# One inverse square root for the norms of four heads' queries and keys

## The chip, the cores and the metric

The kernel runs on one core of one Trainium2 chip. The metric is the time of one execution on the device, in microseconds (us). Five engines matter: PE (TensorE, the matrix engine; PEld is its weight load), DVE (VectorE), ACT (ScalarE), POOL (GpSimd) and SP (SyncE, which here only issues DMA transfers). Each engine works through its own instructions in order, and semaphores between them carry the dependences.

## The reference

The reference is an encoder trunk on 512 positions of width 1024 in float32, with two layers. Layer 0 is a state-space mixer (S5) and a SwiGLU feed-forward block of inner width 2816. Layer 1 has latent attention (MLA) as its mixer, "the second mixer", and another such block. Every block is preceded by an RMS norm that is modulated by a conditioning vector. The part that the change touches is how the attention's heads are made:

```
q = rms_norm(h @ w_dq, q_norm_g) @ w_uq            # 16 heads, 64 + 32 columns each
q_nope = rms_norm(q_nope, q_nope_norm_g)           # over 64 columns of one head
q_rope = apply_rope(rms_norm(q_rope, ...), cos, sin)  # over 32 columns of one head
kv = (c_kv @ w_kv_b)                               # 16 heads, 64 key + 64 value columns
k_nope = rms_norm(k_nope, k_nope_norm_g)           # over 64 columns of one head
rms_norm(x, g) = x * rsqrt(mean(x * x) + 1e-6) * g
```

The scores are masked in chunks of 64 positions, a softmax follows, and the weighted values go through an output projection. For each position and head there are thus three inverse square roots of a mean: of the query's 64 columns, of its 32 rotary columns, and of the key's 64 columns.

## The kernel before

Positions lie in four tiles of 128 partitions. The 16 heads are handled in four groups of four. Products are taken in three passes on PE (high by high, high by low, low by high; `mm3`, lines 923 to 925), so each operand is split into a high part (a cast on ACT) and a low part (a subtraction on DVE, or on POOL for the weights of the head projections, line 164).

The mixer is `mla` (line 1327). A prologue makes the first group: `project` loads its weights, `project_q` and `project_k` multiply and add up squares (DVE reduces at lines 1470, 1471 and 1448, into `hss`), `rotate_q` rotates the raw rotary columns on POOL, `norm_q` and `norm_k` normalize, and `turn` transposes each head's tile on PE and splits it (ACT line 1508, DVE line 1510). In the prologue the two multiplies by the inverse roots of the 64-column norms run on DVE, the rotary one on POOL.

Then a loop over n = 0 to 16 handles one head in each pass. `scores` multiplies queries by keys (PE, lines 1525 to 1527), takes a row minimum on DVE (line 1529) and the exponential on ACT (1530). `scale` divides the rows (DVE 1543, ACT 1541). `spread` transposes the head before and splits it (ACT 930, DVE 931), and `weigh` multiplies it by the values. Into these passes `fill` puts the making of the next group. In its first pass (h = 0, at the end of the pass) come `project`, four `project_q`, `rotate_q` and `norm_q`. In the second pass (h = 1, in front of `weigh`) come four `project_k` and `norm_k`. The third and fourth pass turn the queries and keys. In the loop all three norm multiplies run on POOL (line 158 is the shared helper of multiplies). Group 1 is made beside the attention of group 0, and so on; the traces below have group 1 from about 637 to 679 us, group 2 to 723 us, group 3 to 748 us.

`rsqrt` (line 214) is an inverse square root in integer and float steps on DVE: the mean plus epsilon into `var` (line 1475, once for each kind of norm), a shift (225), a subtraction from a constant (226), and three Newton steps of three instructions (229 to 231). That is 2 + 9 = 11 instructions beside the averages. `norm_q` does it on 32 columns (16 pairs of tile and head, 64-column and rotary norm), `norm_k` on 16. Their scratch tiles come from a pool with one buffer for each tag, "hq" and "hk".

The order of work on each engine is set by a planner when the kernel is built: it takes the instructions with their dependences and places them by its own estimate of their times, so the instructions of one norm stand between those of other work. Besides the data dependences, `issue_after(ins)` puts instructions behind `ins` in their engine's order. `fill` uses it with `self.last`, the rotary multiply of the last query norm: POOL's weight splits of the next group stand behind it. `self.normed` is the last 64-column multiply, used the same way in the prologue.

Of the kernel before, what the change touches and what calls it, by code (L numbers as in the profile page):

```python
# [11 lines left out]
F32 = mybir.dt.float32  # L12
F32R = mybir.dt.float32r
I32 = mybir.dt.int32
# [4 lines left out]
P = 128  # L19
# [6 lines left out]
NOPE = 64  # L26
ROPE = 32
VD = 64
QK = NOPE + ROPE
# [26 lines left out]
class Trunk:  # L56
# [154 lines left out]
        v.tensor_scalar(out=c, in0=cm1, scalar1=1.0, scalar2=None, op0=ALU.add)  # L211
        return s, c, cm1

    def rsqrt(self, pool, ss, n, inv_d, tag):

        v = self.nc.vector
        var = pool.tile([P, n], F32, tag=tag + "v", name=self.name("var"))
        sh = pool.tile([P, n], I32, tag=tag + "s", name=self.name("sh"))
        y = pool.tile([P, n], I32, tag=tag + "y", name=self.name("y"))
        t = pool.tile([P, n], F32, tag=tag + "t", name=self.name("t"))  # L220
        if callable(ss):
            ss(var)
        else:
            v.tensor_scalar(out=var, in0=ss, scalar1=inv_d, scalar2=EPS, op0=ALU.mult, op1=ALU.add)
        v.tensor_scalar(out=sh, in0=var.bitcast(I32), scalar1=1, scalar2=None, op0=ALU.logical_shift_right)
        v.tensor_scalar(out=y, in0=sh, scalar1=-1, scalar2=0x5F3759DF, op0=ALU.mult, op1=ALU.add)
        yf = y.bitcast(F32)
        for _ in range(3):
            v.tensor_tensor(out=t, in0=yf, in1=yf, op=ALU.mult)
            v.scalar_tensor_tensor(out=t, in0=t, scalar=-0.5, in1=var, op0=ALU.mult, op1=ALU.mult)  # L230
            v.scalar_tensor_tensor(out=yf, in0=t, scalar=1.5, in1=yf, op0=ALU.add, op1=ALU.mult)
        return yf
# [1169 lines left out]

    def fill(self, q, h):

        g = self.nc.gpsimd
        if q > 3:
            return
        if h == 0:
            with self.tc.issue_after(self.last.ins):
                self.project(q)  # L1410
            for t in range(4):
                self.project_q(q, t)
            rot = self.tmp.tile([P, 4, 4, ROPE], F32, tag="t0", name=self.name("rot"))
            self.rotate_q(rot)
            self.last = self.norm_q(g, rot)
        elif h == 1:
            for t in range(4):
                self.project_k(q, t)
            self.norm_k(g)
        else:  # L1420
            for j, i in ((0, 1), (1, 1), (2, 1)) if h == 2 else ((0, 0), (1, 0), (2, 0), (3, 1), (3, 0)):
                self.turn(j, i)
# [53 lines left out]
                                            in1=eps.unsqueeze(2).to_broadcast([P, 4, 4]), op0=ALU.mult, op1=ALU.add)  # L1476

    def norm_k(self, eng):
        r = self.rsqrt(self.sm, lambda var: self.mean(var, self.hss[:, 0], self.eps[0], NOPE), 16, None, "hk")
        kn = self.ktm.rearrange("a t h c -> a (t h) c")[:, :, 0:NOPE]  # L1480
        self.normed = self.mul(eng, kn, kn, r.unsqueeze(2).to_broadcast([P, 16, NOPE])).ins

# [3 lines left out]
    def norm_q(self, eng, rot):  # L1486
        v, g = self.nc.vector, self.nc.gpsimd
        qtm, ss = self.qtm, self.hss

        def var(t):  # L1490
            for i, n in enumerate((NOPE, ROPE)):
                self.mean(t[:, 16 * i:16 * i + 16], ss[:, 1 + i], self.eps[1], n)

        r = self.rsqrt(self.sm, var, 32, None, "hq")
        q4 = qtm.rearrange("a t h c -> a (t h) c")
        rb = lambda o, c: r[:, o:o + 16].unsqueeze(2).to_broadcast([P, 16, c])
        self.normed = self.mul(eng, q4[:, :, 0:NOPE], q4[:, :, 0:NOPE], rb(0, NOPE)).ins
        return self.mul(g, q4[:, :, NOPE:QK], rot.rearrange("a t h c -> a (t h) c"), rb(16, ROPE))

    def turn(self, h, i, behind=None):  # L1500

        nc, v = self.nc, self.nc.vector
        src, g = ((self.ktm, self.gk), (self.qtm, self.gq))[i]
        pt = self.ps()
        for t in range(4):
            self.transpose(pt[0:QK, t * P:(t + 1) * P], src[:, t, h], self.ident)
        hi, lo = self.heads[h][i]
        self.last_turn = nc.scalar.activation(out=hi[0:QK], in_=pt[0:QK], func=AF.Copy, scale=g)
        with self.after(behind):
            v.scalar_tensor_tensor(out=lo, in0=pt[0:QK], scalar=g, in1=hi[0:QK].bitcast(F32), op0=ALU.mult, op1=ALU.subtract)  # L1510
# [120 lines left out]
```

## Time and profile before

| | |
|---|---|
| median of 3 runs | 1204.1 us (1202.7 to 1206.66) |
| the profiled execution | 1201.67 us |
| its span, first to last instruction | 1199.9 us |
| mean granted TensorE clock | 0.971 |
| PE, DVE, ACT, POOL busy | 1131.3, 754.3, 491.3, 154.7 us |

The page gives averages over the whole span. A stretch of the span has its own limits, so a row by stretch gives the busy time of each engine in it, beside its length. A group's row adds up the busy time of like instructions: the mean against the time of the shortest tells how much of it is waiting inside instructions. Timelines give single instructions in order: start, duration, engine and line; in brackets, the engine's idle time in front of it and what ended it.

### The profile page before, as it was taken

How to read it: one execution, taken by the hardware profiler on the slowest of the kernel's cores; microseconds unless marked ns; L12 is line 12 of the kernel's file. 1: busy time of each engine (PE TensorE's matmuls, PEld its weight loads, DVE VectorE, ACT ScalarE, POOL GpSimd, SP SyncE). 2: the span in 40 equal slices, each digit the busy share in tenths (PEclk: the TensorE clock that was granted, in tenths of full speed). 3: DMA queues.
4: the chain of work that ended last, by engine and by line, in shares of the span. 5: the costliest groups of instructions: out<-in, count | busy, mean ns of one | idle time of the engine just before them, and what ended most of it. 6: DMA issues, size and time to landing. Idle time of an engine off the chain costs nothing.

```text
span 1199.9 us, 18340 instructions
## 1 busy us (share of the span) xinstructions
PE 1131.3 (94%) x7030; PEld 954.1 (80%) x7030; DVE 754.3 (63%) x1472; ACT 491.3 (41%) x913; POOL 154.7 (13%) x191
## 2 busy tenths in 40 slices
PE   4787898999999999999978988999999999999998
PEld 2565788987777787789967867899978888888888
DVE  8877378598888733756689889768843333322223
ACT  4641465322222322234676868644422322322222
POOL 5997000000000000000143233000000000000000
PEclk7888998999999999999988989999999999999999
DMA  9589965278788732635401021045633333333343
GB/s 266 194 192 198 215 180 157 83 251 260 248 275 261 242 100 84 200 112 173 123 31 36 1 71 36 1 142 167 189 103 102 88 91 103 88 88 104 107 116 105
DMA packets 230072, 167.49 MB, mean 140 GB/s; under 512 B 9776, under 2 KB 204256, under 8 KB 229984
## 3 DMA queue, kind: packets, MB, share of 16 engines
q1 hardware_dynamic: 208904, 128.47, 38.6%
q10 hardware_dynamic: 21080, 37.85, 9.4%
q8 instruction: 55, 0.90, 0.3%
q14 instruction: 33, 0.27, 0.1%
HBM read 163.21 MB, written 3.08 MB: 139 GB/s over the span
## 4 chain that ended last, share of the span: by engine, by line
PE 84%; DVE 9%; ACT 3%; DMA 3%; issue 1%; POOL 0%; SPq 0%; ACTq 0%; DVEq 0%
PE ps L923 24%; PE ps L924 24%; PE ps L925 24%; PE ps L146 2%; DMA a<-in_x 1%; PE ad L811 1%; DVE a L161 1%; DMA adaw<-in_ada_w 1%; PE ac L301 1%; DVE a L158 1%; PE po L924 1%; ACT a L930 1%; PE po L925 1%; DVE a L931 1%; DVE mn L1529 1%
## 5 line engine op out<-in xcount | busy, mean ns | idle before, releaser
L923 PE MATMUL ps<-a,wh 128*128 128x512 f32 (+1 forms) x1406 | 490.0, 353 | 3.7 <-ACT a L996 3.7
L924 PE MATMUL ps<-a,wh 128*128 128x512 f32 (+1 forms) x1406 | 492.2, 352 | 0.6 <-DVE a L997 0.6
L925 PE MATMUL ps<-a,wl 128*128 128x512 f32 (+1 forms) x1406 | 492.3, 352 | 0.0
L912 ACT CAST wh<-raw 128x1024 fp32r<-128x1024 f32 (+1 forms) x179 | 182.6, 1023 | 500.0 <-PE ps L924 359.0
L164 DVE TENSOR_TENSOR wl<-raw,wh 128x1024 fp32r<-128x1024 f32 x173 | 206.6, 1195 | 195.8 <-ACT wh L912 192.5
L923 PEld LDWEIGHTS ps<-a,wh 128*128 128x128 f32 x1406 | 262.9, 189 | 47.0 <-ACT a L996 4.7
L924 PEld LDWEIGHTS ps<-a,wh 128*128 128x128 f32 x1406 | 265.4, 189 | 40.0 <-DVE a L997 0.9
L925 PEld LDWEIGHTS ps<-a,wl 128*128 128x128 f32 x1406 | 265.0, 189 | 39.3 <-DVE wl L164 0.2
L350 DVE SCALAR_TENSOR_TENSOR acc<-a,csil,acc 128x512 f32<-128x512 f32 x126 | 94.5, 750 | 32.4 <-DMA a<-in_ada_w 23.8
L1115 DVE TENSOR_TENSOR si<-si,ps 128x512 f32<-128x512 f32 x44 | 30.1, 685 | 77.4 <-PE ps L925 74.5
L164 POOL TENSOR_TENSOR a<-raw,a 128x768 fp32r<-128x768 f32 (+1 forms) x2 | 4.7, 2356 | 470.1 <-ACT a L912 470.1
L146 PE MATMUL ps<-ident,a 128*128 128x128 f32 (+1 forms) x304 | 47.6, 298 | 18.4 <-POOL a L158 6.6
L146 PEld LDWEIGHTS ps<-ident,a 128*128 128x128 f32 (+1 forms) x304 | 38.1, 146 | 26.1 <-POOL a L158 7.3
L1003 DVE SCALAR_TENSOR_TENSOR xT<-ps,mod,xT 128x256 f32<-128x256 f32 (+1 forms) x35 | 20.4, 583 | 44.5 <-PE ps L925 44.4
L1530 ACT ACTIVATE a<-ps,mn 128x128 f32<-128x128 f32 (+1 forms) x64 | 34.1, 539 | 14.7 <-DVE mn L1529 14.5
L924 PE MATMUL ps<-a,a 128*128 128x256 f32 (+2 forms) x108 | 33.5, 311 | 0.0
L923 PE MATMUL ps<-wh,a 128*128 128x288 f32 (+3 forms) x100 | 33.2, 334 | 0.2 <-DVE a L931 0.2
L923 PE MATMUL ps<-a,a 128*128 128x256 f32 (+2 forms) x108 | 33.1, 313 | 0.0
L1529 DVE TENSOR_REDUCE mn<-ps 128x1 f32<-128x128 f32 (+1 forms) x64 | 30.2, 482 | 4.6 <-PE ps L1527 4.5
L925 PE MATMUL ps<-a,a 128*128 128x256 f32 (+2 forms) x108 | 32.8, 311 | 0.0
L925 PE MATMUL ps<-wh,a 128*128 128x288 f32 (+3 forms) x100 | 32.6, 328 | 0.0
L924 PE MATMUL ps<-wl,a 128*128 128x288 f32 (+3 forms) x100 | 32.4, 325 | 0.0
(324 smaller groups left out, 1458.0 us busy)
## 6 DMA issues: line engine op xcount, KB each, us to landing
a<-in_ada_w ACTq DMA_DIRECT2D x112, 256.0 KB, 4.2
raw<-in_ffn_w_gate SPq DMA_DIRECT2D x44, 512.0 KB, 4.0
raw<-in_ffn_w_up SPq DMA_DIRECT2D x44, 512.0 KB, 5.9
raw<-in_ffn_w_down SPq DMA_DIRECT2D x42, 512.0 KB, 3.8
adaw<-in_ada_w SPq DMA_DIRECT2D x24, 512.0 KB, 8.0
a<-in_ada_w SPq DMA_DIRECT2D x16, 512.0 KB, 7.3
a<-in_kv_ada_w ACTq DMA_DIRECT2D x32, 256.0 KB, 4.1
raw<-in_ffn_w_down SPq DMA_DIRECT2D x21, 384.0 KB, 3.3
```

The lines of the kernel that those rows point to most:

```text
L146: self.nc.tensor.transpose(out=out, in_=in_, identity=ident)
L158: return eng.tensor_tensor(out=out, in0=a, in1=b, op=ALU.mult)
L164: eng.tensor_tensor(out=out, in0=a, in1=b, op=ALU.subtract)
L350: v.scalar_tensor_tensor(out=acc, in0=x, scalar=self.csil[:, k:k + 1], in1=acc, op0=ALU.mult, op1=ALU.add)
L912: nc.scalar.copy(out=flat(wh), in_=flat(raw))
L923: mm(out, lhsT=lhs[0], rhs=rhs[0], start=start, stop=False)
L924: mm(out, lhsT=lhs[0], rhs=rhs[1], start=False, stop=False)
L925: self.last_mm = mm(out, lhsT=lhs[1], rhs=rhs[0], start=False, stop=stop).ins
L1003: self.nc.vector.scalar_tensor_tensor(out=self.xT[:, m, sl], in0=src, scalar=gate[:, m:m + 1], in1=self.xT[:, m, sl], op0=ALU.mult, op1=AL ...
L1115: nc.vector.tensor_tensor(out=t, in0=t, in1=pp[i][1], op=ALU.mult)
L1529: v.tensor_reduce(out=mn[:, t:t + 1], in_=pt, axis=AX.X, op=ALU.min)
L1530: nc.scalar.activation(out=p[:, self.OFF[t]:self.OFF[t] + w], in_=pt, func=AF.Exp, scale=-1.0, bias=mn[:, t:t + 1], accum_out=su[:, t:t + 1])
```

## The change

In the loop, the query norm is no longer done in the first pass. Its rotation stays there, and the rotated columns are kept. In the second pass, after the key projections, one `norm_both` takes three averages into one tile of 48 columns, does one inverse root on it, and then multiplies the queries, the rotary columns and the keys on POOL. `self.last` and `self.normed` are set there. All norms, those of the prologue too, take their scratch tiles from one tag, "hn", as wide as 48 columns.

```diff
-    def rsqrt(self, pool, ss, n, inv_d, tag):
+    def rsqrt(self, pool, ss, n, inv_d, tag, width=0):
-        var = pool.tile([P, n], F32, tag=tag + "v", name=self.name("var"))
+        var = pool.tile([P, width or n], F32, tag=tag + "v", name=self.name("var"))[:, 0:n]
...
     def fill(self, q, h):
...
             for t in range(4):
                 self.project_q(q, t)
-            rot = self.tmp.tile([P, 4, 4, ROPE], F32, tag="t0", name=self.name("rot"))
-            self.rotate_q(rot)
-            self.last = self.norm_q(g, rot)
+            self.rot = self.tmp.tile([P, 4, 4, ROPE], F32, tag="t0", name=self.name("rot"))
+            self.rotate_q(self.rot)
         elif h == 1:
             for t in range(4):
                 self.project_k(q, t)
-            self.norm_k(g)
+            self.norm_both(self.rot)
...
     def norm_k(self, eng):
-        r = self.rsqrt(self.sm, lambda var: ..., 16, None, "hk")
+        r = self.rsqrt(self.sm, lambda var: ..., 16, None, "hn", 48)
...
     def norm_q(self, eng, rot):
-        r = self.rsqrt(self.sm, var, 32, None, "hq")
+        r = self.rsqrt(self.sm, var, 32, None, "hn", 48)
...
+    def norm_both(self, rot):
+        g, ss = self.nc.gpsimd, self.hss
+        def var(t):
+            for i, (e, n) in enumerate(((1, NOPE), (1, ROPE), (0, NOPE))):
+                self.mean(t[:, 16 * i:16 * i + 16], ss[:, (1, 2, 0)[i]], self.eps[e], n)
+        r = self.rsqrt(self.sm, var, 48, None, "hn", 48)
+        q4, k4 = (x.rearrange("a t h c -> a (t h) c") for x in (self.qtm, self.ktm))
+        rb = lambda o, c: r[:, o:o + 16].unsqueeze(2).to_broadcast([P, 16, c])
+        self.mul(g, q4[:, :, 0:NOPE], q4[:, :, 0:NOPE], rb(0, NOPE))
+        self.last = self.mul(g, q4[:, :, NOPE:QK], rot.rearrange("a t h c -> a (t h) c"), rb(16, ROPE))
+        self.normed = self.mul(g, k4[:, :, 0:NOPE], k4[:, :, 0:NOPE], rb(32, NOPE)).ins
```

## Rows read from the trace of the kernel before

**Rows 1.** The page, busy us, share of the span and instructions of each engine.

```profile
PE 1131.3 (94%) x7030; PEld 954.1 (80%) x7030; DVE 754.3 (63%) x1472; ACT 491.3 (41%) x913; POOL 154.7 (13%) x191
```

**Rows 2.** Busy time by stretch: length, engines (instructions), granted clock, DMA share, GB/s.

```profile
core 0: us, PE busy (x) PEld busy (x) DVE busy (x) ACT busy (x) POOL busy (x), PEclk, DMA share, GB/s
636.90:748.00 111.10, 97.62 (x563) 83.32 (x563) 101.44 (x274) 82.64 (x214) 37.93 (x31) 0.94 0.13 39
...
667.80:679.40 11.60, 11.53 (x73) 10.55 (x72) 9.85 (x25) 9.96 (x26) 0.00 (x0) 1.00 0.00 1
...
647.50:658.00 10.50, 6.10 (x32) 4.80 (x32) 10.43 (x23) 4.85 (x13) 6.98 (x4) 0.79 0.34 100
...
688.80:698.50 9.70, 7.26 (x39) 5.70 (x38) 9.70 (x19) 4.42 (x14) 7.96 (x4) 0.80 0.38 114
...
733.00:741.00 8.00, 5.50 (x36) 4.74 (x36) 8.00 (x24) 5.62 (x14) 2.91 (x2) 1.00 0.22 66
```

**Rows 3.** DVE groups by form, 636.9 to 748 us: shapes, count, busy us, mean ns.

```profile
L229 DVE TENSOR_TENSOR t<-y 128x16 f32<-128x16 f32 x9 | 4.6, 515 | 0.1
...
L226 DVE TENSOR_SCALAR y<-sh 128x16 int32<-128x16 int32 x3 | 2.7, 913 | 0.0
L230 DVE SCALAR_TENSOR_TENSOR t<-t,var 128x16 f32<-128x16 f32 x9 | 2.6, 285 | 0.1
...
L231 DVE SCALAR_TENSOR_TENSOR y<-t,y 128x16 f32<-128x16 f32 x9 | 2.3, 257 | 0.0
...
L225 DVE TENSOR_SCALAR sh<-var 128x16 int32<-128x16 int32 x3 | 2.0, 673 | 0.0
```

**Rows 4.** Timeline of DVE, group 1: start us, duration us, instruction, count.

```profile
639.30 0.25 DVE L1475 SCALAR_TENSOR_TENSOR var<-hss,eps_q 128x16 f32<-128x16 f32 x2
...
647.55 0.18 DVE L231 SCALAR_TENSOR_TENSOR y<-t,y 128x32 f32<-128x32 f32 x1
...
648.17 1.65 DVE L1475 SCALAR_TENSOR_TENSOR var<-hss,eps_k 128x16 f32<-128x16 f32 x1
...
652.63 2.27 DVE L229 TENSOR_TENSOR t<-y 128x16 f32<-128x16 f32 x1
...
663.25 0.17 DVE L231 SCALAR_TENSOR_TENSOR y<-t,y 128x16 f32<-128x16 f32 x1
```

**Rows 5.** Timeline of DVE, groups 2 and 3.

```profile
680.84 0.26 DVE L1475 SCALAR_TENSOR_TENSOR var<-hss,eps_q 128x16 f32<-128x16 f32 x2
...
688.73 0.18 DVE L231 SCALAR_TENSOR_TENSOR y<-t,y 128x32 f32<-128x32 f32 x1
688.85 0.18 DVE L1475 SCALAR_TENSOR_TENSOR var<-hss,eps_k 128x16 f32<-128x16 f32 x1
...
707.40 0.17 DVE L231 SCALAR_TENSOR_TENSOR y<-t,y 128x16 f32<-128x16 f32 x1
...
732.85 0.17 DVE L1475 SCALAR_TENSOR_TENSOR var<-hss,eps_k 128x16 f32<-128x16 f32 x1
```

**Rows 6.** Timeline of POOL in the mixer: idle time in front and its releaser in brackets.

```profile
649.74 1.05 POOL L158 TENSOR_TENSOR a<-rot,y 128x512 f32<-128x512 f32 x1
650.74 4.12 POOL L164 TENSOR_TENSOR wl<-raw,wh 128x768 fp32r<-128x768 f32 x2
663.59 1.91 POOL L158 TENSOR_TENSOR a<-a,y 128x1024 f32<-128x1024 f32 x1 [8.73 <-ACT a L930]
...
707.74 1.91 POOL L158 TENSOR_TENSOR a<-a,y 128x1024 f32<-128x1024 f32 x1 [10.72 <-ACT a L1541]
...
743.18 1.90 POOL L158 TENSOR_TENSOR a<-a,y 128x1024 f32<-128x1024 f32 x1 [2.60 <-ACT a L1508]
```

**Rows 7.** Timeline of PE, the key transposes of group 2.

```profile
709.70 2.39 PE L146 MATMUL ps<-ident,a 128*96 128x128 f32 x20 [2.31 <-POOL a L158]
```

**Rows 8.** Line 1543 over the whole span: count, then ns of one, min/median/max.

```profile
L1543 DVE TENSOR_SCALAR a<-a,rc x48: 273/346/933, 636.5 to 770.9; 128x128 f32<-128x128 f32 x16, 128x256 f32<-128x256 f32 x16, 128x384 f32<-128x384 f32 x16
```

**Rows 9.** Timelines of POOL and DVE in the prologue.

```profile
614.59 2.00 POOL L158 TENSOR_TENSOR a<-rot,y 128x512 f32<-128x512 f32 x1 [1.52 <-DVE y L231]
...
620.72 0.17 DVE L226 TENSOR_SCALAR y<-sh 128x16 int32<-128x16 int32 x1
```

More of the change, by code (lines that the diff above doesn't have):

```diff
@@ L212, in sincos @@
         return s, c, cm1
-    def rsqrt(self, pool, ss, n, inv_d, tag):
+    def rsqrt(self, pool, ss, n, inv_d, tag, width=0):
         v = self.nc.vector
-        var = pool.tile([P, n], F32, tag=tag + "v", name=self.name("var"))
-        sh = pool.tile([P, n], I32, tag=tag + "s", name=self.name("sh"))
-        y = pool.tile([P, n], I32, tag=tag + "y", name=self.name("y"))
-        t = pool.tile([P, n], F32, tag=tag + "t", name=self.name("t"))
+        var = pool.tile([P, width or n], F32, tag=tag + "v", name=self.name("var"))[:, 0:n]
+        sh = pool.tile([P, width or n], I32, tag=tag + "s", name=self.name("sh"))[:, 0:n]
+        y = pool.tile([P, width or n], I32, tag=tag + "y", name=self.name("y"))[:, 0:n]
+        t = pool.tile([P, width or n], F32, tag=tag + "t", name=self.name("t"))[:, 0:n]
         if callable(ss):
@@ L1403, in fill @@
     def fill(self, q, h):
-        g = self.nc.gpsimd
         if q > 3:
@@ L1478, in norm_k @@
     def norm_k(self, eng):
-        r = self.rsqrt(self.sm, lambda var: self.mean(var, self.hss[:, 0], self.eps[0], NOPE), 16, None, "hk")
+        r = self.rsqrt(self.sm, lambda var: self.mean(var, self.hss[:, 0], self.eps[0], NOPE), 16, None, "hn", 48)
         kn = self.ktm.rearrange("a t h c -> a (t h) c")[:, :, 0:NOPE]
```

## The prediction

> **What bounds the kernel now.** I read the page first, then the busy time by stretch, the DVE groups by form, and the timelines of DVE, POOL and PE in the second mixer. Over the whole span PE is busy 94% and DVE 63% [rows 1], which would say that DVE work is free. The stage in which the change lies says otherwise. From 636.9 to 748.0 us, where three groups of four heads are projected, normalized and turned beside the attention of the group before, DVE is busy 101.4 of 111.1 us and PE 97.6. The loss is not spread evenly. In a quiet stretch (667.8 to 679.4) PE is busy 11.53 of 11.60 us at full clock. In 647.5 to 658.0, in 688.8 to 698.5 and in 733.0 to 741.0, where a key norm runs, DVE is busy 10.43 of 10.50, 9.70 of 9.70 and 8.00 of 8.00 us, and PE only 6.10, 7.26 and 5.50; the granted clock falls to means of 0.79 and 0.80 (between its two levels of 1.2 and 2.4 GHz) in the first two [rows 2]. So in those stretches DVE is the bound, and its time is worth PE time.
>
> What fills DVE there is partly the code that the change removes. The five lines of the 16-wide inverse root took 4.6+2.7+2.6+2.3+2.0 = 14.2 us for 9+3+9+9+3 = 33 instructions, 0.43 us each [rows 3], though one that runs free takes 0.17 [rows 4]. The excess, 14.2 - 33 x 0.17 = 8.6 us, is stalls: the product at 652.63 took 2.27 us and ended at 654.90 [rows 4], just as POOL's two weight splits ended (650.74 + 4.12 = 654.86) [rows 6]. DVE runs in order, so such a stall also holds the score minima queued behind it, and by them ScalarE and PE.
>
> **The change part by part.** (1) Removed in each of the three groups: one inverse root, 11 DVE instructions, 33 in all. The three averages stay. At free durations that is 33 x 0.17 = 5.6 us of DVE, with the stalls 14.2 us; below, nothing, where DVE has slack. In the prologue (first four heads) both roots stay.
>
> (2) Wider: 33 instructions go from 32 to 48 columns. A 16-wide step takes 0.17 and a 32-wide one 0.18 us [rows 4, 5], so 0.01 to 0.02 us each, at most 0.7 us in all; I take 0.3.
>
> (3) Moved: the query norm waits for the key statistics, and POOL then multiplies query, rotary part and key in a row, 1.91 + 1.05 + 1.91 = 4.87 us [rows 6]. What decides a group is when the last of the three ends, since the key transposes and then the next group's first scores stand behind it; in the second group PE sat idle 2.31 us for exactly this [rows 7]. Before, it ended at 663.59+1.91 = 665.50, 707.74+1.91 = 709.65 and 743.18+1.90 = 745.08 [rows 6]. After, it ends at the key statistics (648.17, 688.85, 732.85, the key averages [rows 4, 5]) plus the length L of the joined chain plus 4.87.
>
> L is not in the trace; its nearest rows are these. The query chain, 13 instructions interleaved with other work, ran from 639.30 to 647.73 (8.4 us) and from 680.84 to 688.91 (8.1 us) [rows 4, 5]. The key chain, 12 instructions, took 648.17 to 663.42 (15.2 us) and 688.85 to 707.57 (18.7 us) [rows 4, 5]. I take the query chain as the nearer: the joined chain starts before POOL has its multiplies and splits to do (they wait for it), so its steps meet none of those, and the query turns, which stood between the steps of the old key chain, can't start before it ends. 14 steps at 8.3/13 are 8.9 us; with the wider steps and one collision I set L = 10. The ends of the range are 8 and 19.
>
> Sum at L = 10: group 1, 648.17+14.87-665.50 = -2.5; group 2, 688.85+14.87-709.65 = -5.9; group 3, 732.85+14.87-745.08 = +2.6, since there the two chains already ran beside each other. Together -5.8 us. The other way of counting, DVE time in full stretches, gives -5.6 without and -14.2 with the stalls, so -5.8 means that few of the stalls come through. What is late next: the query turns, which could start when the rotary multiply ended (649.74+1.05 = 650.79 in group 1 [rows 6]), now start at about 648.2+10+2.96 = 661.1. PE's cover is the weighing of one head and the scores of another; ScalarE and DVE then turn all eight tiles of a group together.
>
> (4) The mark behind which POOL's weight splits of the next group queue (`self.last`) moves with the rotary multiply. At L = 10 they end at 648.2+10+4.87+4.12 = 667.2 in group 1, 13.6 us ahead of the next query average (680.84 [rows 5]): hidden, nothing. If that cover fails, the next projections slip by up to the 4.12 us. The rotated queries' buffer is held longer, one of two, the other free until the next group: nothing. `normed` isn't read in the groups. Nothing changes on the DMA queues but that a raw weight tile comes free some 12 us later; its successors are prefetches of the output weights.
>
> (5) Both prologue norms now share one set of buffers, so the key's `y` waits for POOL's rotary multiply to have read the query's. That ended at 614.59+2.00 = 616.59, and the key's `y` was written at 620.72 [rows 9]: 4.1 us to spare, cost nothing; if DVE reached it at once after its average, at most the POOL multiply, 2.0 us. Behind the waiting instruction on DVE are the rest of the chain and the key turns' halves, for which PE waits.
>
> A rule speaks against a part of this. The row shows a product of two SBUF operands held until POOL was done (2.27 us against 0.17 [rows 4]). The Trainium skill, "SBUF — State Buffer", section "Who interferes with whom", says that VectorE and GpSimd share a port pair as an exclusive lock, and names tensor_scalar among the operations that can contend but says that tensor_reduce never does; the trace agrees on the held product. By that rule the stalls would not vanish but move to whichever DVE instruction meets the now unbroken POOL run; the third rival works that out from rows.
>
> **The rivals.** *The DVE time was covered anyway.* The page's 94% for PE speaks for it; the full DVE stretches speak against. Time: 1204, within 1200.5 to 1207.7. The same comes out if the planner puts the next group's splits ahead of the key multiply: 4.12 us later in the two groups that have splits, -5.8+8.2 = +2.4.
>
> *All stalls go.* 14.2 us off DVE in stretches where it is the bound, and the clock stays up: 1190. Against: group 3 has little to gain.
>
> *The stalls move.* POOL now runs 4.87+4.12 = 9.0 us without a break, across about one head of the softmax. The row scaling there takes 0.35 us at the median and 0.93 at worst [rows 8], so three scalings a head held once each lose up to 3 x 0.6 = 1.8 us, in three groups 5.4: -5.8+5.4 = -0.4, also no change.
>
> *The joined chain is starved (slower).* The planner mixes the steps with the next head's minima and splits, and all 14 must pass before any query or key can be turned. The sum is zero where 3L = (665.50-648.17)+(709.65-688.85)+(745.08-732.85)-3 x 4.87 = 35.8, L = 11.9 us. At L = 15, as the first key chain, it is 3 x (15-11.9) = +9.2, so 1213. For it: both old key chains were longer than 11.9. Against: stalls by POOL made up several us of them.
>
> *It doesn't do what it says.* Only the three later groups change, and the prologue still has two roots; that is in the sum.
>
> **How the numbers follow.** The profiled execution took 1201.67 us (span 1199.9 and 1.8 around it), 2.4 below the median of the runs, 1204.1. The forecast is 1201.67-5.8 = 1195.9 by its own time, and 1204.1-5.8 = 1198.3 by the median, which I give. About 0.3% (3.6 us) is what a measurement tells from no change. Chances: forecast 0.44 (its own range 1192 to 1200.4); all stalls go 0.08; covered or splits first 0.19; stalls move 0.08; starved 0.21. Of the forecast's and the first rival's 0.52 all is faster; 0.27 no change; 0.21 slower. The range 1189 to 1210 leaves out about 0.05 below and 0.1 above.
>
> **What would show it.** In the changed kernel's DVE groups, no 16-wide root outside the prologue, 33 48-wide root steps near 0.2 us each, and busy DVE in the stage down by some 8 us. On POOL, three multiplies in a row in each group, the last ending 12 to 16 us after the key average. PE's idle time in the three bad stretches less, the clock there higher, and the first scores of each next group earlier in groups 1 and 2 and later in group 3. The prediction is wrong if L is above 12 us, if PE waits for POOL's multiplies longer than it waited before, or if DVE's saved time shows up as idle DVE.

## The result: slower, and the profile after

The changed kernel is slower. Its median is 1211.95 us (9 runs, 1204.69 to 1213.99) against 1202.7 us for the kernel before (9 runs, 1199.46 to 1206.66); the ratio is 1.0069 with a 95% interval of 1.0053 to 1.0085 (it is not the quotient of the two medians). So some 8.3 us were lost by the ratio, 9.3 by the medians, where 5.8 were forecast to be won.

The profiled execution took 1208.58 us (span 1206.6, clock 0.969), 6.9 more than the one of before. The loss can be placed by two marks that both traces have: the start of the rotary multiply in the prologue and the first matmul of the output projection. Between them, one row of busy time for each kernel (columns as in [rows 2]); before:

```profile
614.59:775.85 161.26, 139.77 (x817) 121.32 (x817) 145.65 (x376) 121.77 (x305) 43.99 (x34) 0.93 0.11 33
```

and after, with three stretches behind it that answer to the full DVE stretches of [rows 2]:

```profile
616.43:781.69 165.26, 137.20 (x816) 119.74 (x817) 132.03 (x343) 121.10 (x305) 44.57 (x34) 0.92 0.11 32
648.20:658.20 10.00, 5.95 (x35) 4.74 (x35) 6.67 (x25) 4.82 (x13) 3.73 (x3) 0.96 0.00 1
691.50:702.00 10.50, 4.59 (x29) 3.63 (x28) 7.35 (x25) 4.44 (x13) 3.88 (x3) 0.82 0.15 47
735.00:746.00 11.00, 4.90 (x31) 3.94 (x31) 7.47 (x24) 5.12 (x14) 3.25 (x3) 0.85 0.16 48
```

This stretch is 4.0 us longer. Of the rest, 1.8 us arose ahead of it, where the two kernels do the same work, and 0.9 after it. The reader should look at DVE: 33 fewer instructions (376 to 343) and 13.6 us less busy time, in a stretch that nevertheless became longer. In the three stretches behind the key statistics DVE is no longer full (6.67 of 10.00, 7.35 of 10.50, 7.47 of 11.00, against 10.43 of 10.50, 9.70 of 9.70 and 8.00 of 8.00 [rows 2]), and PE, the engine that was to gain, is busy only 5.95, 4.59 and 4.90.

The stalls did go. The groups of the joined root, DVE by form, 638.7 to 749.5 us (answering to [rows 3]):

```profile
L230 DVE SCALAR_TENSOR_TENSOR t<-t,var 128x48 f32<-128x48 f32 x9 | 1.8, 204 | 0.1
L231 DVE SCALAR_TENSOR_TENSOR y<-t,y 128x48 f32<-128x48 f32 x9 | 1.8, 201 | 0.1
L229 DVE TENSOR_TENSOR t<-y 128x48 f32<-128x48 f32 x9 | 1.8, 200 | 0.0
...
L225 DVE TENSOR_SCALAR sh<-var 128x48 int32<-128x48 int32 x3 | 0.5, 178 | 0.0
L226 DVE TENSOR_SCALAR y<-sh 128x48 int32<-128x48 int32 x3 | 0.5, 178 | 0.0
```

Each step takes 0.18 to 0.20 us, none is held by POOL, and the whole joined chain is short. The key average, the last step, and the next DVE instructions that wait, of the three groups (timeline of DVE; idle time in front in brackets):

```profile
647.74 0.17 DVE L1473 SCALAR_TENSOR_TENSOR var<-hss,eps_k 128x16 f32<-128x16 f32 x1
...
654.12 0.21 DVE L231 SCALAR_TENSOR_TENSOR y<-t,y 128x48 f32<-128x48 f32 x1
...
659.28 1.60 DVE L1523 SCALAR_TENSOR_TENSOR a<-ps,gq,a 96x512 fp32r<-96x512 f32 x2 [4.24 <-ACT a L1521]
...
691.09 0.17 DVE L1473 SCALAR_TENSOR_TENSOR var<-hss,eps_k 128x16 f32<-128x16 f32 x1
...
697.78 0.20 DVE L231 SCALAR_TENSOR_TENSOR y<-t,y 128x48 f32<-128x48 f32 x1
...
734.17 0.17 DVE L1473 SCALAR_TENSOR_TENSOR var<-hss,eps_k 128x16 f32<-128x16 f32 x1
...
742.40 0.21 DVE L231 SCALAR_TENSOR_TENSOR y<-t,y 128x48 f32<-128x48 f32 x1
...
747.56 1.60 DVE L1523 SCALAR_TENSOR_TENSOR a<-ps,gq,a 96x512 fp32r<-96x512 f32 x2 [4.95 <-ACT a L1521]
```

So L was 6.6, 6.9 and 8.4 us, shorter than the 10 of the forecast. What follows on POOL in group 1 (timeline, answering to [rows 6]):

```profile
654.47 1.90 POOL L158 TENSOR_TENSOR a<-a,y 128x1024 f32<-128x1024 f32 x1 [11.15 <-DVE y L231]
656.33 1.05 POOL L158 TENSOR_TENSOR a<-rot,y 128x512 f32<-128x512 f32 x1
657.34 1.90 POOL L158 TENSOR_TENSOR a<-a,y 128x1024 f32<-128x1024 f32 x1
659.20 4.17 POOL L164 TENSOR_TENSOR wl<-raw,wh 128x768 fp32r<-128x768 f32 x2
```

and on PE in the three groups (timeline, answering to [rows 7]):

```profile
653.42 0.27 PE L925 MATMUL po<-a,a 128*128 128x128 f32 x1
...
657.44 2.79 PE L146 MATMUL ps<-ident,a 128*96 128x128 f32 x12 [3.74 <-POOL a L158]
659.88 0.46 PE L1538 MATMUL ps<-a 100*128 100x128 f32 x1
...
701.93 2.80 PE L146 MATMUL ps<-ident,a 128*96 128x128 f32 x12 [5.42 <-POOL a L158]
...
745.71 2.80 PE L146 MATMUL ps<-ident,a 128*96 128x128 f32 x12 [5.29 <-POOL a L158]
```

PE has finished the weighing at 653.7, and the next thing in its order is the query transposes, which need both query multiplies; the scores of the next head stand behind them (659.88). It waits until the rotary multiply ends at 657.38. With no scores there are no minima for DVE and no exponentials for ScalarE: from 655.04 to 657.40 PE, DVE and ACT are busy 0.00 us and POOL all of it. Before, the corresponding row of group 3 was this:

```profile
740.64 1.51 PE L146 MATMUL ps<-ident,a 128*96 128x128 f32 x12 [1.24 <-POOL a L158]
```

The same twelve transposes took 1.51 us there and 2.79 to 2.80 after the longer waits. The granted clock of just these rows, group 3 before and then after (length, PE busy, clock, DMA share, GB/s):

```profile
740.64:742.15 1.51, 1.51 (x14) 1.00 0.00 0
745.71:748.51 2.80, 2.80 (x14) 0.50 0.00 0
```

It was 0.50, the lower of the two levels (1.2 of 2.4 GHz), in groups 1 and 2 of the changed kernel too. In group 3 the longer wait thus cost 1.3 us more than its own length. In groups 1 and 2 the kernel before had slow transposes as well (0.90 us for four at 694.37, clock 0.60), so there this is not a new cost. Where the 4.0 us arose is seen from the last group, from its first rotation on POOL to the output projection, before and after (columns as in [rows 2]):

```profile
723.09:775.85 52.76, 48.72 (x310) 41.82 (x308) 49.01 (x131) 42.36 (x112) 10.22 (x9) 1.00 0.07 21
724.53:781.69 57.16, 49.91 (x309) 43.41 (x308) 46.61 (x120) 42.34 (x112) 10.18 (x9) 0.94 0.07 19
```

This part is 4.4 us longer, at a clock of 0.94 instead of 1.00, with 3.2 us more in which PE is idle and 1.2 more in which it is busy; groups 1 and 2 together are 0.4 us shorter.

### The profile page after: what moved, and what is told of

Same layout as the page of the kernel before. It is cut to its first block, busy times and chain, and to the rows that moved or that the text cites. A ratio compares the mean times of both kernels' runs of the same rounds, so it can differ in the third digit from the quotient of the medians.

```text
span 1206.6 us, 18313 instructions
## 1 busy us (share of the span) xinstructions
PE 1131.9 (94%) x7030; PEld 954.7 (79%) x7030; DVE 739.3 (61%) x1439; ACT 491.0 (41%) x913; POOL 155.3 (13%) x191
## 4 chain that ended last, share of the span: by engine, by line
PE 81%; DVE 8%; DMA 4%; ACT 3%; issue 2%; SPq 1%; POOL 0%; POOLq 0%; ACTq 0%; DVEq 0%
PE ps L923 24%; PE ps L924 24%; PE ps L925 24%; PE ps L146 2%; DMA a<-in_x 1%; DVE a L931 1%; DVE a L161 1%; DVE a L158 1%; PE ac L301 1%; DMA raw<-in_w_kv_b 1%; DMA a<-kd 1%; ACT a L1543 1%; DVE mn L1542 1%; ACT a L930 1%; PE po L924 1%
```

## The experiments

The theory (A in the expectations): the query norm now starts only behind the last key statistic, and POOL's multiplies come behind that, so the queries are ready too late for PE, and the gain on DVE falls into time in which DVE stands anyway. The rivals: it is the joined chain or its shared scratch, or the loss is not on POOL at all. All ratios are to the kernel before on the same chip and, as above, are not quotients of the medians; the fourth column is the stretch between the two marks in that run's one profile, the last the sum of PE's waits for POOL in front of transposes from 620 to 790 us (e6 has 3.1 us more in front of them, for the multiply that it does on DVE).

| kernel | median us | ratio (95%) | stretch us | PE for POOL us |
|---|---|---|---|---|
| before | 1202.7 | 1 | 161.3 | 3.6 |
| changed | 1211.95 | 1.0069 (1.0053 to 1.0085) | 165.3 | 14.4 |
| e1 turns late | 1207.3 | 1.0055 (1.0037 to 1.0073) | 165.3 | 2.2 |
| e2 two roots, late | 1209.07 | 1.0054 (1.0031 to 1.0077) | 167.0 | 15.6 |
| e3 shared scratch only | 1204.73 | 1.0021 (0.9999 to 1.0042) | 162.7 | 6.1 |
| e4 no query multiply | 1200.22 | 0.9984 (0.9968 to 1.0001) | 158.5 | 8.9 |
| e5 rotary twice | 1216.62 | 1.0137 (1.0107 to 1.0168) | 176.7 | 22.3 |
| e6 query multiply on DVE | 1204.8 | 1.0026 (1.0004 to 1.0049) | 161.1 | 8.1 |
| e7 short key root | 1195.9 | 0.9950 (0.9928 to 0.9973) | 153.6 | 1.2 |
| e8 splits behind | 1197.33 | 0.9975 (0.9955 to 0.9995) | 154.9 | 1.2 |
| e9 e8, query on DVE | 1205.93 | 1.0026 (1.0017 to 1.0035) | 164.4 | 4.2 |

One execution's stretch moves by more than the medians do, so verdicts rest on the ratios, and the profiles only show where the time lies.

**e2, the move without the joining.**

```diff
-            rot = self.tmp.tile(...)
-            self.rotate_q(rot)
-            self.last = self.norm_q(g, rot)
+            self.rot = self.tmp.tile(...)
+            self.rotate_q(self.rot)
...
                 self.project_k(q, t)
+            with self.tc.issue_after(self.key_sum):   # the last key statistic on DVE
+                self.last = self.norm_q(g, self.rot)
             self.norm_k(g)
```

> Kernel of before with two separate roots and their own scratch tiles, but the query root and its multiplies moved behind the last key statistic, where the changed kernel has its joined root. This leaves only the move, without the joining. Theory A: the move is what costs, so PE waits for POOL before the query turns as in the changed kernel (three waits of 3 to 7 us), and the 33 instructions that are back on DVE add 0 to 6 us: 1211 to 1218, ratio 1.007 to 1.015. Rival D (the joined chain, its width or its shared scratch, is what costs): back to before, 1201 to 1205, ratio 0.998 to 1.002.

Measured 1.0054: rival D is excluded, the move alone gives a loss of this size. The 33 instructions that are back on DVE cost nothing that the intervals show beside the changed kernel (1.0031 to 1.0077 against 1.0053 to 1.0085), a little less than theory A had set for them. PE's waits for POOL (total, times, longest), and the row between the two marks:

```profile
PE ps L146 <- POOL a L158: 15.6, 3, 5.8
613.41:780.37 166.96, 138.46 (x816) 120.56 (x817) 133.94 (x376) 121.37 (x305) 44.80 (x34) 0.93 0.11 32
```

With all 376 instructions DVE is busy 133.94 us, against 145.65 before and 132.03 in the changed kernel. So 11.7 of the 13.6 us by which DVE's busy time fell came with the move, which takes the steps away from POOL's work, and 1.9 with the 33 instructions.

**e3, the shared scratch alone.** The kernel of before with the "hn" tags.

> Kernel of before with one change: the scratch tiles of query and key roots share one set of buffers, 48 wide, as in the changed kernel. Theory A: the sharing costs nothing by itself where a wait is already satisfied, ratio 0.998 to 1.002; but in the groups, where key and query chains of one group run beside each other before, sharing can make the key chain wait for POOL's multiplies of the query, so up to +3 us there (1.000 to 1.003). Rival C (the sharing is the loss): 1.005 to 1.009.

Measured 1.0021 (0.9999 to 1.0042): rival C is excluded as the whole loss. Whether sharing costs anything in this kernel stays open within that interval; it could, since two chains are under way in a group there. In the changed kernel a group has one chain, and in its prologue the key's `y` comes as late behind the rotary multiply as before.

**e4, POOL's query multiply left out; e5, its rotary multiply doubled; e6, the query multiply on DVE.** In `norm_both`:

```diff
 e4
-        self.mul(g, q4[:, :, 0:NOPE], q4[:, :, 0:NOPE], rb(0, NOPE))
 e5
+        self.mul(g, q4[:, :, NOPE:QK], rot.rearrange("a t h c -> a (t h) c"), rb(16, ROPE))
         self.last = self.mul(g, q4[:, :, NOPE:QK], rot.rearrange("a t h c -> a (t h) c"), rb(16, ROPE))
 e6
-        self.mul(g, q4[:, :, 0:NOPE], q4[:, :, 0:NOPE], rb(0, NOPE))
+        self.mul(self.nc.vector, q4[:, :, 0:NOPE], q4[:, :, 0:NOPE], rb(0, NOPE))
```

> The changed kernel without POOL's multiply of the queries' 64 columns in the three groups of the loop (these queries stay unnormalized); the root and the two other multiplies stay. Theory A: the query turns wait for POOL 1.9 us less in each group, three times 1.9 = 5.7 us come off the waits and most of it off the time: 4 to 7 us faster than the changed kernel, 1205 to 1208, ratio 1.001 to 1.004. Rival B (POOL's place in the chain is covered, the loss sits on DVE or in the order): unchanged, 1209 to 1214.

> The changed kernel with POOL's rotary multiply done twice in each of the three groups (same operands, same result), so the chain behind the joined root is 1.05 us longer in each. Theory A (POOL's multiplies behind the late root are exposed one for one or more): the three waits of PE grow by 1.05 each, stage between the prologue's rotary multiply and the first output projection 165.3 -> 168 to 170 us, median 1213 to 1217, ratio to before 1.009 to 1.013. Rival B (POOL is covered; the run without the query multiply gained for another reason): as the changed kernel, 1.005 to 1.0085.

> The changed kernel with the queries' 64-column multiply of the three groups on DVE instead of POOL. DVE stood idle 4 to 5 us there in each group of the changed kernel; the multiply took 1.23 us on DVE in the prologue, where POOL's rotary multiply beside it took 2.00 instead of 1.05. Theory A: query ready about 2.1 us behind the root instead of 2.95, keys 4.0 instead of 4.85: 0.9 us less wait in each group, 3 to 5 us off the stage in sum, ratio 1.002 to 1.005. Rival E (the pair contends for the port so that nothing is won): as the changed kernel, 1.006 to 1.008.

All three went theory A's way, and rivals B and E are out. e4 and e5 moved more than was set. For e5 the trace says why: the planner put the key multiply between the two rotary ones (timeline of POOL, group 1):

```profile
650.21 1.90 POOL L158 TENSOR_TENSOR a<-a,y 128x1024 f32<-128x1024 f32 x1 [11.12 <-DVE y L231]
652.07 1.05 POOL L158 TENSOR_TENSOR a<-rot,y 128x512 f32<-128x512 f32 x1
653.07 1.90 POOL L158 TENSOR_TENSOR a<-a,y 128x1024 f32<-128x1024 f32 x1
654.93 1.05 POOL L158 TENSOR_TENSOR a<-rot,y 128x512 f32<-128x512 f32 x1
```

so the queries were ready some 2.9 us later, not 1.05. By the time from the root's last step to the first query transpose, the four kernels stand in order. In group 1 it is 1.28 us in e4 (654.45 to 655.73), 2.45 in e6 (654.56 to 657.01), 3.11 in the changed kernel (654.33 to 657.44) and 5.96 in e5 (650.07 to 656.03); over the three groups 4.6, 6.9, 10.2 and 18.9 us. The ratios rise with it: 0.9984, 1.0026, 1.0069, 1.0137. From e4 to the changed kernel 5.6 us of delay cost 0.85% (10.2 us), from there to e5 8.7 us cost 0.68% (8.2 us): by this estimate each microsecond of lateness costs about one to two. The clock is a part of the first step only in group 1, where e4's transposes took 1.51 us after a wait of 1.91; in its other groups they took 2.79, as in the changed kernel. The rest of what e4 won above its expectation is not explained. Even with no query multiply at all the late root is barely at par with the kernel before.

**e1, the turns moved instead.**

```diff
-            for j, i in ((0, 1), (1, 1), (2, 1)) if h == 2 else ((0, 0), (1, 0), (2, 0), (3, 1), (3, 0)):
+            for j, i in () if h == 2 else ((0, 1), (1, 1), (2, 1), (0, 0), (1, 0), (2, 0), (3, 1), (3, 0)):
```

> The changed kernel, but all eight turns of a group are called in the fourth pass, after that pass's scores, instead of three query turns in the third. Theory A: the time is lost because PE, which works in order, has the query transposes in front of the next head's scores, and stands 3.7 to 5.4 us in each group until POOL's query and rotary multiplies are done; with the scores in front PE has work there, the three waits (14.5 us in the profile of the changed kernel) shrink to under 5 in sum, and the kernel is faster than the changed one by 5 to 12 us, so 1200 to 1207, ratio to before 0.997 to 1.004. Rival B (the loss is the late query norm itself, whatever PE does in between, since eight turns must pass before the next group's first scores): no gain or worse, 1210 to 1216. Rival C (shared scratch tiles or another part of the change): unchanged, 1209 to 1214.

PE's waits for POOL fell as theory A said (14.4 to 2.2 us), but the ratio, 1.0055, overlaps the changed kernel's: no gain is shown, and the part of theory A that put it all on PE's order fell. With the next head's softmax running beside POOL's unbroken run, its DVE work met that run (timeline of DVE, group 2):

```profile
700.86 2.17 DVE L164 TENSOR_TENSOR wl<-raw,wh 128x1024 fp32r<-128x1024 f32 x1
...
703.04 0.99 DVE L931 TENSOR_TENSOR a<-ps,a 128x384 fp32r<-128x384 f32 x2
703.95 6.21 DVE L1556 TENSOR_SCALAR a<-a,rc 128x128 f32<-128x128 f32 x3
710.08 2.05 DVE L1523 SCALAR_TENSOR_TENSOR a<-ps,gq,a 96x512 fp32r<-96x512 f32 x3
```

while POOL did this:

```profile
701.91 2.03 POOL L158 TENSOR_TENSOR a<-rot,y 128x512 f32<-128x512 f32 x1
703.90 1.90 POOL L158 TENSOR_TENSOR a<-a,y 128x1024 f32<-128x1024 f32 x1
705.76 4.18 POOL L164 TENSOR_TENSOR wl<-raw,wh 128x768 fp32r<-128x768 f32 x2
```

Three row scalings took 6.21 us (0.88 in the changed kernel, 711.42), to just behind the end of POOL's second split at 709.94; the splits of PSUM tiles beside them were not held (0.99 us for two). In groups 1 and 3 the three scalings took 3.68 and 4.79 us, so some 12 us were lost in the three groups, as much as DVE's busy time in the stretch grew (144.51 us against 132.03). PE's waits for the split of line 931, which stands behind held work, grew from 2.0 to 7.7 us. That is the third rival of the prediction, in a kernel in which work does stand beside POOL. So the late multiplies cost time either way; that the held scalings are what took e1's gain is read from its profile, and no run without them was made. The Trainium skill, "SBUF — State Buffer", section "Who interferes with whom", has it that tensor_scalar can contend with GpSimd for the shared port pair, and that a DVE instruction with at most one SBUF input, outside the 2-port modes, does not; the trace agrees with both, by 6.21 us for the scalings and 0.99 us for the splits.

**e7, the DVE work alone.** The kernel of before, without the nine Newton instructions of the key root in the loop (the keys are scaled by the first guess).

```diff
-            self.norm_k(g)
+            self.norm_k(g, 0)          # number of Newton steps; the prologue keeps 3
```

> Kernel of before, without the nine Newton instructions of the key root in the three groups of the loop (the keys are scaled by the first guess): 27 DVE instructions of 16 columns less, nothing moved. This prices the DVE work that the change removes, without the delay of the queries. Theory A: the work was worth what the forecast took, 3 to 9 us: 1194 to 1200, ratio 0.992 to 0.998. Rival F (the DVE work was covered, so that the change had nothing to gain from the start): 0.999 to 1.002.

Measured 0.9950 (0.9928 to 0.9973): taking 27 such instructions out where they stand is worth 6.0 us, so rival F is out. That is the size of the forecast's gain, but not the price of DVE time alone. DVE's busy time in the stretch fell by only 3.3 us (145.65 to 142.38), and with a shorter chain the keys are ready sooner: group 1's key multiply starts 40.1 us behind the prologue's rotary multiply (656.53), against 49.0 before (663.59), and PE's waits for POOL fall from 3.6 to 1.2 us. How the 6.0 us divide between the two is not shown.

**e8, a version from the same stalls.**

```diff
-            with self.tc.issue_after(self.last.ins):
+            with self.tc.issue_after(self.last.ins if q == 1 else self.behind):
                 self.project(q)
...
             self.norm_k(g)
+            self.behind = self.normed
```

> Kernel of before, with the weight splits of groups 2 and 3 queued on POOL behind the key multiply instead of the rotary multiply, so that the key root's steps don't meet them. If the stalls of DVE on POOL's splits (2.27 and 1.26 us in group 1, 1.30 and 1.20 in group 2) held the stage up, 2 to 5 us faster than before: ratio 0.996 to 0.999; if the splits come late for the next projections, or the stalls were covered, 0.999 to 1.003.

Measured 0.9975 (0.9955 to 0.9995), faster than the changed kernel and, by an interval that only just leaves out 1, than the kernel before. The queries stay early, and the key root's steps no longer meet POOL's splits; its chain in group 1, key average and last step:

```profile
649.37 1.63 DVE L1476 SCALAR_TENSOR_TENSOR var<-hss,eps_k 128x16 f32<-128x16 f32 x1
...
660.07 0.16 DVE L231 SCALAR_TENSOR_TENSOR y<-t,y 128x16 f32<-128x16 f32 x1
```

10.9 us instead of 15.2 [rows 4]; the average still meets the query multiply, and three row scalings now meet the key multiply and the splits (4.68 us at 662.21).

**e9, e8 with the query multiply on DVE.** `self.norm_q(g, rot)` of `fill` becomes `self.norm_q(self.nc.vector, rot)`.

> Kernel of before with the weight splits behind the key multiply (as the run that beat the kernel before) and the queries' 64-column multiply of the three groups on DVE. For it: queries are ready about 0.9 us sooner and POOL is free of 1.9 us beside the key root's first steps (the key average held 1.6 us there). Against: 1.23 us of DVE in each group where DVE is full. If POOL's hold on the key root is worth more than the DVE time: 1191 to 1196, ratio 0.990 to 0.996; otherwise 0.997 to 1.001, no better than the splits alone (0.9975).

Measured 1.0026 (1.0017 to 1.0035): the second branch, and worse than it set, by 0.5% (6 us) against e8. The multiply is 1.2 us of DVE in each group, but the 6 us are not its price alone. In all three groups the row scalings now stand beside POOL's key multiply, and in two of them beside its splits; in group 1 (timeline of DVE):

```profile
660.29 4.14 DVE L1544 TENSOR_SCALAR a<-a,rc 128x128 f32<-128x128 f32 x3
```

In groups 2 and 3 they took 4.15 and 2.52 us, where in e8 only group 1's were held. The part of the multiply and that of these holds were not separated.

## Why the prediction was wrong, point by point

**What bounds the stage: right as a description, incomplete as a bound.** DVE was full behind the key statistics, and e7 shows that taking work from the key chain there is worth time. But it was full because the queries were ready early, which let scores, turns and the key root overlap.

**Step 1, removed work: near in size by luck, and lost.** 33 instructions went and DVE's busy time in the stretch fell by 13.6 us, near the 14.2 of the upper bound. But e2, with all 33 back, has 11.7 of these 13.6 us too: it was the move that ended the stalls. None of it came through, and e2 is no slower. DVE's saved time became idle time, 33.2 us between the marks against 15.6, one of the three signs of being wrong that the prediction names; PE's longer waits for POOL (14.4 us against 3.6) are another.

**Step 2, widening: right in kind, somewhat small.** The 33 steps took 6.4 us, 0.8 more than at 0.17 each, where 0.3 and at most 0.7 was set.

**Step 3, the move: the step that failed.** L was mis-sized on the safe side (10 forecast, 6.6, 6.9 and 8.4 measured), so by the step's own sum the kernel should have won 13.9 us (35.8 - 21.9). What failed is its premise, "What decides a group is when the last of the three ends", taken from the one wait of [rows 7]. The last multiply did end sooner behind the key average (659.24-647.74 = 11.5 us in group 1, against 665.50-648.17 = 17.3), and the group didn't end sooner. What decided was the first query transposes: from the key average to them it was 3.9, 5.5 and 7.8 us before, and 9.7, 10.8 and 11.5 after. Those of groups 1 and 2 before (timeline of PE; group 3's, 740.64, is shown above):

```profile
652.05 0.60 PE L146 MATMUL ps<-ident,a 128*96 128x128 f32 x4
694.37 0.90 PE L146 MATMUL ps<-ident,a 128*96 128x128 f32 x4 [1.67 <-ACT a L1530]
```

The text named this ("What is late next: the query turns") and then covered it with "the weighing of one head and the scores of another". Only the weighing was there; in the planner's order the scores stand behind the query transposes. The uncovered part is the three waits of 14.4 us. The trace of before held the sign: in group 3 the query transposes already waited 1.24 us for POOL. Groups 1 and 2 broke even on it (from one group's first rotation to the next, 42.3 and 43.5 us, 42.5 and 43.7 before): there DVE's busy time fell by 7.6 and 3.9 us. Group 3, where it fell by only 2.4, took the loss: 57.2 us to the output projection against 52.8.

**Steps 4 and 5: right.** The splits came well ahead of their use, and the prologue's key chain ran as before.

**The rivals.** The starved chain gave the nearest time (1213), but by a mechanism that didn't occur: the chain stayed below the forecast's 10 us in every group. Its 0.21 stood for the outcome, not for the cause, and the range, which ended at 1210 with 0.1 above it, had no room for this rival's 1213. (The 0.52 for "faster" are the forecast and *all stalls go*, which stands second in the list.) The stalls that move were seen in e1, e8 and e9, not in the changed kernel, where the longest row scaling took 0.42 us against 0.93 before: DVE had nothing there to hold.

What stays open: the ratio stands for 8.3 us, the two profiled executions differ by 6.9 and their stretches by 4.0. Of the remainder 1.8 us lie ahead of the stage, where the code is the same, and the changed kernel's profiled execution was 3.4 us below the median of its runs.

## What to carry to other kernels

Before merging two small chains to save instructions on a busy engine, look at what the earlier of them releases: the saving is worth its time only where it leaves the earlier result early. Cover has to be checked in the waiting engine's own order, since work that is ready but stands behind the waiting instruction covers nothing. Where a small chain is slow because another engine holds its steps, moving that other engine's work behind the chain (e8) got some gain without the delay; what that work meets in its new place has to be looked at again.

## What was not expected of the hardware

A wait of PE could cost more than its length: the twelve query transposes took 1.51 us at a granted clock of 1.00 after 1.24 us of waiting, and 2.79 to 2.80 us at 0.50 after 3.74 to 5.42 us. And POOL's unbroken multiplies and splits could hold three short DVE scalings for 6.21 us, which is seven times their own 0.88 us.
